# RWKV score products in quarter-array tiles: halves of the weights' tokens, and K against A and r in one product

## The chip, the cores and the metric

One core of one Trainium2 chip runs the whole model: four layers on one sequence of 256 tokens with 2048 channels. The metric is the device time of one execution in microseconds. The kernel before was run three times: 2886.83 us in the median, 2881.13 to 2887.49.

## The reference, cut to what matters

Layers 0 and 3 are RWKV-7 mixers with 32 heads of 64 channels, layer 1 is gated linear attention, layer 2 a state-space mixer. The change touches the RWKV mixer alone. Its recurrence is

```
def step(state, inp):
    r_t, k_t, v_t, w_t, kk_t, a_t = inp
    removal = jnp.einsum('bhvk,bhk->bhv', state, kk_t)
    state = (state * w_t[:, :, None, :]
             - jnp.einsum('bhv,bhk->bhvk', removal, kk_t * a_t)
             + jnp.einsum('bhv,bhk->bhvk', v_t, k_t))
    return state, jnp.einsum('bhvk,bhk->bhv', state, r_t)
```

The kernel computes it in two chunks of 128 tokens. Within a chunk it needs, for each head, four 128 x 128 matrices of products between tokens, each a sum over the head's 64 channels: the removal rows against the removal columns (B with A), B with r, K with A and K with r, where A, B, K and R are the four scaled vectors that the code keeps in one tile, `abkp`.

## The kernel before, in words

All activations lie transposed: channels on the 128 partitions, 256 tokens along the free axis. The large projections (`proj`, `jobs`, `prods`, line 393) take a 512 KB block of weights at a time, split it into a high and a low part (ScalarE line 338, VectorE line 340) and make three products of 256 columns for each 128 x 128 block into the PSUM tile `acc`. They fill most of the time of TensorE.

An RWKV layer goes through its 2048 channels in 8 units of 256 channels, that is of 4 heads. A unit holds two tiles of 128 channels (index q), each with two heads (index h: partitions 0 to 63 and 64 to 127), and two chunks of 128 tokens (index c). Two stages matter here, each running beside a projection:

- `rwkv_first` (beside the projection to k) makes A, B and K, writes them to DRAM, and calls `gram` once for B with A: four entries, (c, q). VectorE scales the result into `LT` (line 769), and `unit_inverse` inverts it with many small products (lines 982 to 1024).
- `rwkv_second` (beside the projection to r) loads A, B, K and the decay back into `abkp`, multiplies r into the fourth part (line 807), and calls `gram` three times: once for B with R (four entries, (c, q); masked on VectorE at line 823) and once for each chunk in `prep` for K with A and R (four entries: A q0, A q1, R q0, R q1; masked at line 845). The masked matrices `G` are the weights of the products at lines 864, 891 and 892.

`gram` (line 776) takes a two-bank PSUM tile, one bank for each h. For each entry and each h it issues one float32 product (line 785): the 64 channels of the head are the contracted rows, 128 tokens of s are the weights, 128 tokens of t are the moving columns. One call is 8 products; the trace shows two weight loads and two matmul records for each float32 product, so 16 records. There are 4 calls in a unit, 8 units in a layer and 2 such layers: 64 calls.

The source's order isn't the order of the queues: the Tile framework schedules the whole program with `schedule_with_timeline_sim=True`, so products of different parts are mixed on TensorE's queue by priority and by the times that its planner assumes. Semaphores are set from the data. A call of `gram` can so be cut into several pieces with other products between them. DMA traffic of this part is on GpSimd's queue (loads of `abkp`, `rv`, `Tt`) and SyncE's (stores); the weight blocks are on SyncE's.

Of the kernel before, what the change touches and what calls it, by code (L numbers as in the profile page):

```python
# [129 lines left out]
class Kern:  # L130
# [555 lines left out]
    def rwkv_first(self, i, j, un, kps, lora, ra):  # L686
# [7 lines left out]
        NCH, C, H = 2, 128, 64  # L694
# [5 lines left out]
        def v2(t):  # L700
            return t[:, 0:512].rearrange("p (q t) -> p q t", q=2)
# [7 lines left out]
        kT, tha, S = abk[:, 0, :], abk[:, 1, :], abk[:, 2, :]  # L709
# [4 lines left out]
        for n, (nm, dst, b) in enumerate((("dec", thd, self.hw0), ("iclr", tha, self.ha0))):  # L714
            ps = self.b1()
            for q in range(2):
                nc.tensor.matmul(ps[:, q * T:(q + 1) * T], w2[0:LORA, n, q * P:(q + 1) * P], lora[nm][0:LORA],
                                 start=True, stop=True)
# [20 lines left out]
        ps = self.b1()  # L739
# [25 lines left out]
        Lf = ra.tile([P, 8 * C + 16], F32, name="LT", bufs=3)  # L765
        nc.gpsimd.memset(Lf[:, 8 * C:], 0.0)
        LT = Lf[:, 0:8 * C].rearrange("p (m t) -> p m t", t=C)
        for h, g in enumerate(self.gram([(v2(tha), v2(kT), c, q) for c in range(NCH) for q in range(2)])):
            nc.vector.tensor_tensor(out=LT[:, 4 * h:4 * h + 4, :], in0=g,
                                    in1=n2[:, 4 * h:4 * h + 4].unsqueeze(2).broadcast_to([P, 4, C]), op=ALU.mult)  # L770
        Tt = self.unit_inverse(LT, Lf, ra)
# [4 lines left out]
    def gram(self, which):  # L776


        C, H = 128, 64
        both = self.g2()  # L780
        ps = [both[:, h, :] for h in range(2)]
        for n, (s, t, c, q) in enumerate(which):
            for h in range(2):
                r = slice(H * h, H * h + H)
                self.nc.tensor.matmul(ps[h][:, n * C:(n + 1) * C], s[r, q, c * C:(c + 1) * C], t[r, q, c * C:(c + 1) * C],  # L785
                                      start=True, stop=True)
        return [p.rearrange("p (n t) -> p n t", t=C) for p in ps]

    def rwkv_second(self, i, j, un, spill, kept, rb, last):
# [3 lines left out]
        NCH, C, H = 2, 128, 64  # L793
# [3 lines left out]
        abkp = rb.tile([P, 4, 2, T], F32, name="abkp")  # L797
        nc.gpsimd.dma_start(out=abkp, in_=kept[0].rearrange("p w (q t) -> p w q t", q=2))
        Ac, Bc, Kc, Rc = (abkp[:, w] for w in range(4))
# [12 lines left out]
        ps = self.b1()  # L812
# [4 lines left out]
        def Gt():  # L817
            return rb.tile([P, 4, C], F32, name="G", bufs=7)

        GBR = []  # L820
        for h, g in enumerate(self.gram([(Bc, Rc, c, q) for c in range(NCH) for q in range(2)])):
            GBR.append(Gt())
            nc.vector.tensor_tensor(out=GBR[h], in0=g, in1=self.c("kmask", C).unsqueeze(1).broadcast_to([P, 4, C]),
                                    op=ALU.mult)
        def prep(c):


            tk = rb.tile([P, 3, 2, P], F32, name="tk", bufs=3)
            for w0, ws in ((0, (Bc, Kc)), (2, (vT,))):
                if w0 == 0 and c == NCH - 1:  # L830
                    continue
                ps = self.b1()
                for w, src in enumerate(ws):
                    for q in range(2):
                        o, t = ps[:, (2 * w + q) * P:(2 * w + q + 1) * P], src[:, q, c * C:(c + 1) * C]
                        if w0 == 2:
                            nc.tensor.matmul(o, t, self.c("cen"), start=True, stop=True)
                        else:
                            nc.tensor.transpose(o, t, self.c("ident"))
                n = len(ws)  # L840
                nc.scalar.copy(out=tk[:, w0:w0 + n, :, :].rearrange("p w q t -> p (w q t)"), in_=ps[:, 0:n * 2 * P])
            G = []
            for h, g in enumerate(self.gram([(Kc, t, c, q) for t in (Ac, Rc) for q in range(2)])):
                G.append(Gt())
                nc.vector.tensor_tensor(out=G[h].rearrange("p (w q) t -> p w q t", w=2),
                                        in0=g.rearrange("p (w q) t -> p w q t", w=2),
                                        in1=self.c("kmask").rearrange("p (w t) -> p w t", w=2).unsqueeze(2)
                                        .broadcast_to([P, 2, 2, C]), op=ALU.mult)
            return tk, G
        first = prep(0)  # L850
        yield

        yb = self.b3()
        St = self.St[un % 2]
        for c in range(NCH):
            tk, G = prep(c) if c else first
            ps = self.b2()
            for q in range(2):
                if c:
                    nc.tensor.matmul(ps[:, q * P:(q + 1) * P], Ac[:, q, c * C:(c + 1) * C], St[:, q].rearrange("p h v -> p (h v)"),  # L860
                                     start=True, stop=False)
                for h in range(2):
                    n = 2 * q + h
# [3 lines left out]
            ps = self.b2()  # L867
# [6 lines left out]
            if c < NCH - 1:  # L874
                ps = self.b2()
                for n, (q, h) in enumerate(QH):
                    o = ps[HS[h], q * H:(q + 1) * H]
# [6 lines left out]
            for q in range(2):  # L884
# [3 lines left out]
                for h in range(2):  # L888
                    n = 2 * q + h
                    o = yb[:, c * T + n * H:c * T + (n + 1) * H]  # L890
# [12 lines left out]
        ps = self.b1()  # L903
# [562 lines left out]
```

## Time and profile before

| what | value |
|---|---|
| median of three runs | 2886.83 us (2881.13 to 2887.49) |
| the profiled execution's own time | 2881.41 us |
| its span, first to last instruction | 2879.4 us |
| TensorE busy (matmul) | 2691.4 us, 93% |
| VectorE busy | 2213.7 us, 77% |
| ScalarE busy | 1392.7 us, 48% |
| mean granted TensorE clock, 1 is 2.4 GHz | 0.959 |

The profiled execution is 5.4 us (0.19%) under the median of the runs. Busy time counts a stretch once even where records overlap. A matmul record reaches some 0.2 us beyond its stream of columns, so the pace of products is read from starts: from the start of a group to the start of the next.

### The profile page before, as it was taken

The page shows a single profiled execution, that of the slowest core. Times are in us where ns is not written, and L with a number is a line of the kernel's source. Part 1 is how long each engine was busy: PE and PEld are TensorE (multiplying, and loading weights), DVE is VectorE, ACT ScalarE, POOL GpSimd, SP SyncE. Part 2 cuts the span into 40 slices and gives each one's busy share as a digit, 9 for nine tenths or more (in the row PEclk, how much of TensorE's full clock was granted, in tenths as well). Part 3 has the DMA queues.
Part 4 walks back from the last instruction along what each step waited for, and adds up shares of the span by engine and source line. Part 5 has one row for each costly group of instructions (what it writes and reads, how often), then busy time and mean ns, then how long its engine had stood idle before and what let it go on. Part 6 is the DMA issues. An engine that isn't in the chain of part 4 may idle for free.

```text
span 2879.4 us, 62022 instructions
## 1 busy us (share of the span) xinstructions
PE 2691.4 (93%) x25074; PEld 2533.2 (88%) x25074; DVE 2213.7 (77%) x3918; ACT 1392.7 (48%) x2315; POOL 153.8 (5%) x298
## 2 busy tenths in 40 slices
PE   6899899999977999998998999999889989999997
PEld 4789899998967899987898999999779989899997
DVE  5778777878788988877888787887678888565666
ACT  3475655333335544444544454554357666452333
POOL 0011110101000000000000000000001011110100
PEclk8899889999998999999999999999999989999999
DMA  9876558978586888975775767666557765684633
GB/s 341 313 239 198 165 162 285 352 270 293 178 287 222 315 296 295 321 257 196 280 264 191 233 221 232 220 212 223 180 170 242 228 197 184 194 299 160 206 118 114
DMA packets 239118, 673.55 MB, mean 234 GB/s; under 512 B 72272, under 2 KB 78416, under 8 KB 235760
## 3 DMA queue, kind: packets, MB, share of 16 engines
q1 hardware_dynamic: 217904, 580.84, 59.8%
q0 software_dynamic: 20928, 88.75, 8.6%
q8 instruction: 197, 3.23, 0.5%
q14 instruction: 89, 0.73, 0.1%
HBM read 620.66 MB, written 48.82 MB: 233 GB/s over the span
## 4 chain that ended last, share of the span: by engine, by line
PE 72%; DVE 10%; DMA 10%; issue 3%; ACT 2%; SPq 2%; POOL 0%; DVEq 0%; ACTq 0%; POOLq 0%
PE acc L393 56%; DMA raw<-in_ada_w 3%; DVE L L340 3%; PE g L785 2%; PE pv L393 2%; DVE adaacc L304 2%; ACT H L338 1%; DMA raw<-in_rwkv_w_in 1%; DMA raw<-in_rwkv_w_out 1%; DMA dx<-bd 1%; PE b L892 1%; PE b L869 1%; DMA raw<-in_gla_w_in 1%; PE b L891 1%; PE b L864 1%
## 5 line engine op out<-in xcount | busy, mean ns | idle before, releaser
L393 PE MATMUL acc<-xs,H 128*128 128x256 f32 x8480 | 1631.3, 291 | 32.0 <-ACT H L338 8.4
L393 PEld LDWEIGHTS acc<-xs,H 128*128 128x128 f32 x8480 | 1359.7, 196 | 61.7 <-ACT H L338 10.9
L393 PE MATMUL acc<-xs,L 128*128 128x256 f32 x4240 | 1228.9, 290 | 18.2 <-DVE L L340 17.9
L338 ACT CAST H<-raw 128x1024 fp32r<-128x1024 f32 (+1 forms) x706 | 718.2, 1018 | 862.0 <-PE acc L393 636.1
L340 DVE TENSOR_TENSOR L<-raw,H 128x1024 fp32r<-128x1024 f32 (+1 forms) x706 | 834.1, 1184 | 249.0 <-ACT H L338 233.9
L393 PEld LDWEIGHTS acc<-xs,L 128*128 128x128 f32 x4240 | 828.3, 195 | 31.9 <-DVE L L340 23.4
L304 DVE SCALAR_TENSOR_TENSOR adaacc<-raw,cact,adaacc 128x1024 f32<-128x1024 f32 x300 | 384.0, 1280 | 111.5 <-DMA raw<-in_ada_w 109.5
L393 PE MATMUL acc<-ys,H 128*128 128x256 f32 x1536 | 292.2, 290 | 10.1 <-DVE ys L409 3.8
L393 PEld LDWEIGHTS acc<-ys,H 128*128 128x128 f32 x1536 | 244.7, 194 | 20.7 <-issue 7.4
L393 PE MATMUL acc<-ys,L 128*128 128x256 f32 x768 | 221.1, 288 | 0.0
L393 PEld LDWEIGHTS acc<-ys,L 128*128 128x128 f32 x768 | 149.0, 194 | 3.2 <-issue 3.2
L551 ACT ACTIVATE hn<-x,mod,omu 128x256 f32<-128x256 f32 x192 | 113.4, 599 | 2.9 <-DVE xm L554 1.4
L431 DVE SCALAR_TENSOR_TENSOR x<-acc,mod,x 128x256 f32<-128x256 f32 x192 | 83.7, 478 | 33.3 <-PE acc L393 33.1
L393 PE MATMUL acc<-H,xs 128*128 128x256 f32 x512 | 97.4, 290 | 0.9 <-ACT vt L1072 0.7
L554 DVE SCALAR_TENSOR_TENSOR xm<-x,par,hn 128x256 f32<-128x256 f32 x192 | 88.9, 478 | 1.4 <-ACT hn L551 0.3
L393 PEld LDWEIGHTS acc<-H,xs 128*128 128x128 f32 x512 | 82.7, 198 | 2.5 <-issue 1.2
L393 PE MATMUL acc<-L,xs 128*128 128x256 f32 x256 | 73.7, 289 | 0.0
L785 PE MATMUL g<-abkp 64*128 64x128 f32 x768 | 68.6, 294 | 1.8 <-DVE abkp L807 1.7
L408 ACT CAST xs<-xm 128x256 fp32r<-128x256 f32 x128 | 50.9, 400 | 34.1 <-DVE xm L554 31.8
L785 PEld LDWEIGHTS g<-abkp 64*128 64x128 f32 x768 | 53.4, 189 | 14.2 <-issue 6.2
L1278 DVE SCALAR_TENSOR_TENSOR cva<-cvp,hcw,cva 128x256 f32<-128x256 f32 x144 | 65.1, 478 | 0.0
L278 DVE SCALAR_TENSOR_TENSOR adaacc<-raw,cact,adaacc 128x512 f32<-128x512 f32 x56 | 42.0, 749 | 28.1 <-DMA raw<-in_ada_w 23.4
(358 smaller groups left out, 3138.4 us busy)
## 6 DMA issues: line engine op xcount, KB each, us to landing
raw<-in_ada_w SPq DMA_DIRECT2D x384, 512.0 KB, 4.9
raw<-in_rwkv_w_in SPq DMA_DIRECT2D x256, 512.0 KB, 4.8
raw<-in_ssd_w_in SPq DMA_DIRECT2D x128, 512.0 KB, 4.3
raw<-in_gla_w_in SPq DMA_DIRECT2D x96, 512.0 KB, 5.2
raw<-in_ssd_w_out SPq DMA_DIRECT2D x64, 512.0 KB, 4.0
raw<-in_rwkv_w_out SPq DMA_DIRECT2D x48, 512.0 KB, 4.4
abkp<-kd POOLq DMA_DIRECT2D x16, 1024.0 KB, 7.8
raw<-in_gla_w_out SPq DMA_DIRECT2D x32, 512.0 KB, 4.9
```

Source lines behind the costliest of these rows:

```text
L278: nc.vector.scalar_tensor_tensor(out=acc, in0=raw[:, u, :], scalar=self.cact[:, k:k + 1], in1=acc, op0=ALU.mult, op1=ALU.add)
L304: nc.vector.scalar_tensor_tensor(out=acc, in0=raw, scalar=self.cact[:, k:k + 1], in1=acc, op0=ALU.mult, op1=ALU.add)
L338: nc.scalar.copy(out=hi, in_=raw[:, a:a + n])
L340: nc.vector.tensor_tensor(out=lo, in0=raw[:, a:a + n], in1=hi, op=ALU.subtract)
L393: self.nc.tensor.matmul(ps, lhs, rhs, start=first and part == 0 and w is hi, stop=last and w is lo)
L408: nc.scalar.copy(out=t[:, 0, :], in_=src)
L431: nc.vector.scalar_tensor_tensor(out=self.x[:, t, 1:], in0=ps[:, u, :], scalar=gate[:, t:t + 1], in1=self.x[:, t, 1:], op0=ALU.mult, op1=A ...
L551: nc.scalar.activation(t1, x[:, k, 1:], AF.Identity, scale=self.omu[:, col:col + 1], bias=self.mods[(i, 0)][:, k:k + 1])
L554: done[k] = nc.vector.scalar_tensor_tensor(out=xm, in0=x[:, k, 0:T], scalar=self.p("rwkv_mu", col), in1=t1, op0=ALU.mult, op1=ALU.add)
L785: self.nc.tensor.matmul(ps[h][:, n * C:(n + 1) * C], s[r, q, c * C:(c + 1) * C], t[r, q, c * C:(c + 1) * C], start=True, stop=True)
L864: nc.tensor.matmul(ps[:, n * H:(n + 1) * H], G[h][:, q, :], tk[:, 2, q, HS[h]], start=not c, stop=not c or h == 1)
L1278: nc.vector.scalar_tensor_tensor(out=a, in0=src[:, k:k + T], scalar=w[k], in1=a, op0=ALU.mult, op1=ALU.add)
```

## The change

`gram` now gives every product a quarter of the array. Before, an entry was two products, one for each head, with 128 tokens of s as weights. Now it is four: for each head (h, the contracted rows) and each half of s's tokens (u, 64 weights' columns and 64 output partitions). The order is (u, h) = (0, 0), (1, 1), (1, 0), (0, 1). Output banks and places are as before: bank h, partitions by u.

The moving side gets one more axis, so that one product can stream several parts of `abkp`. For K with A and R, `abkp[:, 0::3]` is parts 0 and 3, and a product has 2 x 128 = 256 moving columns; the entries go from four to two. For B with A and B with R the axis has length 1 and a product keeps its 128 columns.

So a call for K has 2 x 4 = 8 products of 64 rows x 64 weights' columns with 256 moving columns (before: 8 of 64 x 128 with 128). A call for B with A or with R has 4 x 4 = 16 products of 64 x 64 with 128 moving columns (before: 8 of 64 x 128 with 128). Nothing else is edited.

```diff
-        for h, g in enumerate(self.gram([(v2(tha), v2(kT), c, q) for c in range(NCH) for q in range(2)])):
+        for h, g in enumerate(self.gram([(v2(tha), v2(kT).unsqueeze(1), c, q) for c in range(NCH) for q in range(2)])):
...
         for n, (s, t, c, q) in enumerate(which):
-            for h in range(2):
-                r = slice(H * h, H * h + H)
-                self.nc.tensor.matmul(ps[h][:, n * C:(n + 1) * C], s[r, q, c * C:(c + 1) * C], t[r, q, c * C:(c + 1) * C],
-                                      start=True, stop=True)
+            for u, h in ((0, 0), (1, 1), (1, 0), (0, 1)):
+                r, o = slice(H * h, H * h + H), slice(H * u, H * u + H)
+                tr = t[r, :, q, c * C:(c + 1) * C]
+                nt = tr.shape[1]
+                to = ps[h][o].rearrange("p (w n t) -> p w n t", w=nt, t=C)[:, :, n, :]
+                self.nc.tensor.matmul(to, s[r, q, c * C + H * u:c * C + H * u + H], tr, start=True, stop=True)
...
-        for h, g in enumerate(self.gram([(Bc, Rc, c, q) for c in range(NCH) for q in range(2)])):
+        for h, g in enumerate(self.gram([(Bc, abkp[:, 3:4], c, q) for c in range(NCH) for q in range(2)])):
...
-            for h, g in enumerate(self.gram([(Kc, t, c, q) for t in (Ac, Rc) for q in range(2)])):
+            for h, g in enumerate(self.gram([(Kc, abkp[:, 0::3], c, q) for q in range(2)])):
```

## Rows read from the trace of the kernel before

**Rows 1.** The page's busy times and its chain that ended last, by engine.

```profile
PE 2691.4 (93%) x25074; PEld 2533.2 (88%) x25074; DVE 2213.7 (77%) x3918; ACT 1392.7 (48%) x2315; POOL 153.8 (5%) x298
...
PE 72%; DVE 10%; DMA 10%; issue 3%; ACT 2%; SPq 2%; POOL 0%; DVEq 0%; ACTq 0%; POOLq 0%
```

**Rows 2.** Busy time by stretch: the RWKV stages of both layers, and their sum.

```profile
520.00:840.00 320.00, 303.79 (x2643) 286.21 (x2642) 249.87 (x421) 100.84 (x158) 26.39 (x48) 0.98 0.76 271
...
2470.00:2790.00 320.00, 313.44 (x3294) 294.24 (x3295) 202.87 (x381) 122.22 (x207) 35.28 (x66) 0.99 0.59 200
sum 1070.00, PE 1024.49 PEld 964.77 DVE 784.26 ACT 478.67 POOL 112.20; mean PE 256.12 PEld 241.19 DVE 196.06 ACT 119.67 POOL 28.05
```

**Rows 3.** Line 785 (gram): its matmul records, and their busy time over the same stretches.

```profile
L785 PE MATMUL g<-abkp x768: 272/272/579, 522.4 to 2782.9; 64*128 64x128 f32 x192
...
L785 PE MATMUL g<-abk x256: 272/272/580, 232.0 to 2450.1; 64*128 64x128 f32 x128
...
sum 1070.00, PE 84.97 PEld 66.49; mean PE 21.24 PEld 16.62
```

**Rows 4.** Timeline of TensorE: gram in one piece, and a piece of eight.

```profile
530.25 0.97 PEld L785 LDWEIGHTS g<-abkp 64*128 64x128 f32 x16
530.25 1.16 PE L785 MATMUL g<-abkp 64*128 64x128 f32 x16
...
531.34 0.39 PE L393 MATMUL acc<-xs,L 128*128 128x256 f32 x1
...
524.68 0.71 PE L785 MATMUL g<-abkp 64*128 64x128 f32 x8
525.32 0.38 PE L393 MATMUL acc<-xs,L 128*128 128x256 f32 x1
```

**Rows 5.** Timeline of TensorE: the state-space layer's products in two column halves (128*64).

```profile
1426.49 0.39 PE L1362 MATMUL b<-M,xc 128*64 128x128 f32 x4
...
1427.80 0.39 PE L1362 MATMUL b<-M,xc 128*64 128x128 f32 x4
...
1428.67 1.09 PE L1364 MATMUL b<-ce,xd 128*64 128x128 f32 x16
1429.69 0.39 PE L393 MATMUL acc<-xs,L 128*128 128x256 f32 x1
```

**Rows 6.** Timeline of TensorE: float32 products of 256 columns, whole array and four column quarters.

```profile
523.00 0.70 PE L814 MATMUL b<-rv,cst 128*128 128x256 f32 x2
523.63 0.48 PE L785 MATMUL g<-abkp 64*128 64x128 f32 x2
...
502.64 0.64 PE L310 MATMUL mx<-adaacc,cst 128*32 128x256 f32 x8
503.20 0.39 PE L393 MATMUL acc<-xs,H 128*128 128x256 f32 x1
```

**Rows 7.** Timeline of TensorE: 32*32 products with the same rows, mixed, and one kind alone.

```profile
299.85 0.19 PE L1012 MATMUL b<-P,T 32*32 32x32 f32 x1
...
300.20 0.19 PE L1012 MATMUL b<-P,T 32*32 32x32 f32 x1
300.32 0.38 PE L393 MATMUL acc<-xs,H 128*128 128x256 f32 x1
...
303.26 0.69 PE L1010 MATMUL b<-T,P 32*32 32x32 f32 x16
303.88 0.38 PE L393 MATMUL acc<-xs,L 128*128 128x256 f32 x1
```

**Rows 8.** Who reads gram's result, who waits for it, and who waits for line 807.

```profile
L845 DVE TENSOR_TENSOR G<-g,cst x64: 675/681/692, 534.9 to 2783.9; 128x512 f32<-128x512 f32 x64
...
PE g L785: 14.4, 17
...
PEld g L785: 2.2, 3
PE g L785: 1.7, 2
```

## The prediction

> **What bounds the kernel now.** I read the page first, then the stretches, then line 785 by itself, then the timeline product by product. The page shows an engine that is nearly full: TensorE is busy 93% of the span and holds 72% of the chain that ended last [rows 1]. In the four RWKV stretches that contain every call of gram it is fuller still, 1024.5 of 1070 us or 96%, with VectorE at 73% [rows 2]. So time saved on TensorE there should come through at about 0.95 of its size, and time added costs the same share. The granted clock is 0.98 and 0.99 in the two long stretches [rows 2], which is the upper level, 2.4 GHz, nearly throughout; I take all durations at that level.
>
> Gram has 768 + 256 = 1024 matmul records and 85.0 us of busy time [rows 3]. How that splits is read from two pieces. Sixteen records go from 530.25 to the next product's start at 531.34, 1.09 us; eight go from 524.68 to 525.32, 0.64 us [rows 4]. The difference, 0.45 us for eight records, is 56 ns for each record, and what is left, 1.09 - 16 x 0.056 = 0.19 us, is paid once for each piece: the first weight load, and the emptying of the array before the next kind of product. The busy times of the two pieces, 1.16 and 0.71 us, are 0.26 us over the same 56 ns for each record. So 85.0 = 1024 x 0.056 + pieces x 0.265, which gives 104 pieces for the 64 calls: some calls are cut by other products, 40 times in all.
>
> **The change, part by part.**
>
> *The work itself.* The array does as many multiplications as before. A record of 128 columns in half the array (64 x 128) becomes two in a quarter, or one in a quarter with twice the columns. A gain can only come from the way the tiles fill and empty, and a loss if quarters don't run side by side.
>
> *Do column halves run side by side?* The state-space layer has float32 products of 128 columns in column halves (128*64). From 1426.49 to 1427.80, six groups of four records pass in 1.31 us, 54.6 ns for each [rows 5], the pace that two at a time give, as in gram. Sixteen in one piece take 1428.67 to 1429.69, 1.02 us; less 16 x 0.0546 that is 0.15 us for the piece. Against gram's 0.19 this is 0.04 us less, and the difference I put down to the first load, which has 64 columns of weights in place of 128.
>
> *Do four run side by side, with 256 columns?* On the whole array two records of 256 columns take 523.00 to 523.63, 0.63 us, that is about 0.20 us for the piece and 0.216 for each. In four column quarters eight records take 502.64 to 503.20, 0.56 us [rows 6]: two rounds of 0.216 and 0.13 for the piece. Four records cost what one costs.
>
> *Do two run side by side that share their rows?* This is what gram never did: (u, h) = (0, 0) and (1, 0) both read partitions 0 to 63. The nearest rows are the 32*32 products of the inverse. Lines 1010 and 1012 both contract partitions 32 to 63, into different PSUM partitions. From 299.85 to 300.20 twelve of line 1012 pass, with twelve of line 1010 between them; that is eleven intervals in 0.35 us, 32 ns for a pair. Line 1010 alone takes 303.26 to 303.88, 0.62 us for sixteen; less about 0.12 for the piece, 31 ns for one [rows 7]. So two tiles with the same rows pass in the time of one. The trace has no 64*64 case of this, so I keep both ends: side by side, as these rows show, or two at a time, which doubles the rounds.
>
> *A call for K* (32 of them) becomes four rounds of four records of 256 columns: 0.15 + 4 x 0.216 + 0.02 for the staggered start of four = 1.03 us, against 1.09. *A call for B with A or R* (32) becomes eight rounds of four records of 128: 0.15 + 8 x 0.109 + 0.02 = 1.04 us. The saving is 0.06 and 0.05 us, together 3.5 us if each call is one piece. The 40 further pieces each get the shorter load less the stagger, 0.02 us, 0.8 us. That is 4.3 us on TensorE, and 4.1 at 0.95. The other end of the unknown: with two at a time a call takes 4 x 0.216 or 8 x 0.109 us more, 0.87, and 64 calls 56 us.
>
> *What is added.* The 32 calls for B have 8 more products each, 512 more records and as many loads. They stream beside the others and are in the sum above; their issue has no row of its own, and the 32*32 rows, at 16 ns for each record [rows 7], bound it under the 27 ns that a quarter of a round of 109 ns leaves. Nothing in DMA, ScalarE or VectorE is added or moved: the masks of line 845 keep their 0.68 us for the same 128 x 512 [rows 8].
>
> *The new wait.* A product of K with A now waits for line 807 as well, since it streams R with it. Behind it on TensorE's queue would stand the projection. B with R comes first in the same unit and waits for line 807 already; TensorE's waits for that line are 2.2 + 1.7 us in the whole span [rows 8]. I take nothing for it; if that cover went, it could double these, at most 4 us.
>
> *Latency.* VectorE stood idle 14.4 us in 17 stops for gram [rows 8]. Each now ends 0.05 us earlier, 0.9 us at most.
>
> **The sum** is 4.1 + 0.9 = 5.0 us. From the profiled execution's 2881.4 us that is 2876.4. That execution lies 5.4 us under the median of the runs, so against the median of 2886.8 I expect **2882 us**, 0.17% less. A measurement of this kernel can tell some 0.2%, 5.8 us, from no change, so the forecast lies just inside what can't be told.
>
> *A rule that speaks against it.* If a weight load could not pass beside a running product of the same rows, gram before would already take a load and a product in turn. It doesn't: its sixteen loads take 0.97 us in all, and the products follow at 56 ns each, 112 for two in parallel, although in each half every load has the same rows as the product ahead of it [rows 4]. The Trainium skill, in "TensorE: Matmul & The Clock Gate", Part 3, under what overlaps and what doesn't, says that a weight load overlaps with products in flight only when the row groups differ. By that rule, the trace disagrees before the change; it would have to hold for quarter tiles alone.
>
> **The rivals.**
>
> *The pieces become fewer or more.* The planner sets the order anew for the whole program, with twice the products in the calls for B and longer ones in the calls for K. For fewer speaks that a call for K has two entries in place of four, so fewer places to cut. If all 40 cuts went, at 0.17 us each (0.15 + 0.02), 7 us more would be saved: 2882 - 7 = **2875 us**.
>
> *Cuts that leave quarters alone* (the other side). A call for K that is cut after one product runs two records of 256 columns with three quarters of the array empty. That costs 0.17 for the piece and 2 x 0.216 for rounds hardly filled, 0.6 us, where a cut before cost 0.19 and at most two records' 0.11. Against the 5 us saved and the 5.8 that can be told, it decides from 18 such cuts in the 32 calls; one in each would give 2882 + 19 = **2901 us**. For it speaks that 40 cuts exist now; against it, that the busy time of the pieces fits full pairs closely, so cuts mostly fall between entries.
>
> *Tiles with the same rows run in turn.* Then 56 x 0.95 = 53 us are added: **2935 us**. Only that no 64*64 pair was seen speaks for it; rows 7 speak against it.
>
> *Loads are not hidden in quarter tiles.* Each round would then show its load of 64 columns. From rows 4 and 5, 64 columns less cost 0.04 us of the fixed part, so I take 0.05: 32 x 8 + 32 x 4 = 384 rounds, 19 us, **2900 us**. By the Trainium skill's rule above this is what would come.
>
> *Nothing comes through.* Where the projection beside gram waits for VectorE or for a weight block, TensorE's 4 us are lost again: **2887 us**. TensorE's 96% speaks against it.
>
> **How the numbers follow.** The forecast has 0.50: its own range is 2876 to 2888, by what a new order of the queues moves (one cut is 0.17 us, a few waits of the projection 1 us each); of this 0.16 falls beyond 0.2% faster, 0.33 within, 0.01 slower. Fewer pieces 0.22, faster. Lonely quarters 0.12, of which 0.11 slower and 0.01 within. The same rows in turn 0.05, slower. Loads not hidden 0.05, slower. Nothing comes through 0.06, within. Together: faster 0.38, within 0.40, slower 0.22. The range goes from 2871 (no cuts left and a few waits gone) to 2901, which takes in the loads and the lonely quarters; what is left out is the 2935 us and the tails, under 2 in 10.
>
> **What would show it.** Right: line 785 has 512 + 512 records of 128 columns and 512 of 256, all 64*64; an uncut call for K lasts about 1.03 us to the next product's start and an uncut call for B 1.04, with starts in fours; busy time of the line falls under 85 us; TensorE's share in the RWKV stretches stays at 96%. Wrong: an uncut call near 1.9 us (turns), near 1.3 for K and 1.5 for B (loads), or calls near 1.03 us in more than 120 pieces with the line's busy time above 90 us. If calls last what I say and the time still moves by more than 10 us, the cause is the order of the other work, which my sum doesn't hold.

## The result, and the profile after

The changed kernel takes 2909.63 us in the median of four runs (2908.33 to 2914.86), the kernel before 2885.12 beside it (2881.13 to 2887.49): a ratio of 1.0093, with a 95% interval of 1.0068 to 1.0118. It is 24.5 us slower. The forecast was 2882, its range ended at 2901, and slower had a chance of 0.22: the prediction was wrong in its sign and its range. The profiled execution after took 2908.33 us with a span of 2906.0.

The page after, where it answers to [rows 1]; then the two costliest lines of TensorE (busy, mean ns, idle ahead of them and its main releaser):

```profile
span 2906.0 us, 63046 instructions
...
PE 2697.5 (93%) x25586; PEld 2519.3 (87%) x25586; DVE 2211.1 (76%) x3918; ACT 1392.7 (48%) x2315; POOL 154.0 (5%) x298
...
PE 70%; DVE 12%; DMA 11%; issue 4%; ACT 2%; SPq 1%; POOL 0%; DVEq 0%; ACTq 0%; POOLq 0%
...
L393 PE MATMUL acc<-xs,H 128*128 128x256 f32 x8480 | 1634.4, 291 | 40.3 <-DVE xs L409 10.4
...
L393 PE MATMUL acc<-xs,L 128*128 128x256 f32 x4240 | 1232.1, 291 | 21.3 <-DVE L L340 21.1
```

TensorE has the 512 further records (25586 against 25074) and 6.1 us more busy time, about a quarter of the 26.6 us by which the span grew; the other 20.5 us are idle time of TensorE (208.5 us for 188.0). In the chain TensorE has two points less, VectorE two and DMA one more: there is more waiting. The projection's own two groups waited 40.3 and 21.3 us; before, 32.0 and 18.2. The mean granted clock of the span is 0.954, before 0.959.

**Where the time went.** The same two stretches (first RWKV layer; the two middle layers) of the kernel before, and then of the kernel after. The columns are the stretch, its length, busy time and instructions of PE, PEld, DVE, ACT and POOL, then the granted clock, the DMA share and GB/s.

```profile
200.00:1000.00 800.00, 746.63 (x7518) 697.47 (x7518) 638.87 (x1119) 379.69 (x665) 62.83 (x119) 0.96 0.73 248
1000.00:2200.00 1200.00, 1143.77 (x9276) 1094.17 (x9276) 963.65 (x1600) 586.25 (x871) 13.32 (x22) 0.97 0.70 237
```

```profile
200.00:1000.00 800.00, 733.66 (x7600) 672.35 (x7598) 618.96 (x1093) 370.27 (x648) 62.74 (x119) 0.94 0.70 237
1000.00:2200.00 1200.00, 1143.68 (x9272) 1093.10 (x9273) 965.29 (x1597) 580.34 (x858) 12.27 (x20) 0.97 0.70 240
```

In the middle layers TensorE's busy time is the same to a tenth of a microsecond. In the first stretch every engine is busy for less of the 800 us, at a granted clock of 0.94 for 0.96. I set the two traces side by side by the k-th product of the projection's line 393, which has 16416 in both: product 1200 comes 2.6 us later after the change (258.5 for 255.9), product 1600 17.2 us (363.5 for 346.3), product 2800 27.3 us (613.5 for 586.2). At the end it is 26.5. For four fifths of the products between, the difference is 22 to 27 us; for short stretches, in the two RWKV layers above all, it moves out to 18 or 40. So in these two executions nearly all is lost in the first RWKV layer, and most of it before the second stage.

**The tiles themselves did what they should.** Line 789 (gram) after: records, shortest, median and longest in ns, first and last start, shapes of some.

```profile
L789 PE MATMUL g<-abkp x1024: 269/376/685, 538.7 to 2803.2; 64*64 64x128 f32 x86, 64*64 64x256 f32 x85
...
L789 PE MATMUL g<-abk x512: 269/269/418, 233.9 to 2465.5; 64*64 64x128 f32 x171
```

Timeline of TensorE after: a call for B in one piece, a call for K in one piece, and a call for K in two (start, busy, line, tiles, count).

```profile
263.15 1.10 PE L789 MATMUL g<-abk 64*64 64x128 f32 x32
264.18 0.39 PE L393 MATMUL acc<-xs,L 128*128 128x256 f32 x1
...
550.48 1.09 PE L789 MATMUL g<-abkp 64*64 64x256 f32 x16
551.50 0.39 PE L393 MATMUL acc<-xs,L 128*128 128x256 f32 x1
...
616.71 0.66 PE L789 MATMUL g<-abkp 64*64 64x256 f32 x6
617.30 0.66 PE L909 MATMUL b<-cst,ysq 128*128 128x128 f32 x4
```

A call for B takes 264.18 - 263.15 = 1.03 us, a call for K 551.50 - 550.48 = 1.02, against 1.09 for both in [rows 4]. Cut, the call for K pays 0.59 us for six records, and the other ten, further on, 1.00 (not shown here): 1.59 instead of 1.02.

### The profile page after: what moved, and what is told of

The parts are those of the page before. It is cut to its first block, busy times and chain, and to the rows that moved or that the text cites. A ratio compares the mean times of both kernels' runs of the same rounds, so it can differ in the third digit from the quotient of the medians.

```text
span 2906.0 us, 63046 instructions
## 1 busy us (share of the span) xinstructions
PE 2697.5 (93%) x25586; PEld 2519.3 (87%) x25586; DVE 2211.1 (76%) x3918; ACT 1392.7 (48%) x2315; POOL 154.0 (5%) x298
## 4 chain that ended last, share of the span: by engine, by line
PE 70%; DVE 12%; DMA 11%; issue 4%; ACT 2%; SPq 1%; POOL 0%; DVEq 0%; ACTq 0%; POOLq 0%
PE acc L393 55%; DMA raw<-in_ada_w 5%; DVE L L340 3%; DVE adaacc L304 2%; PE pv L393 2%; PE g L789 2%; DMA raw<-in_rwkv_w_in 1%; ACT H L338 1%; DMA raw<-in_gla_w_in 1%; PE b L895 1%; DMA raw<-in_rwkv_w_out 1%; PE b L894 1%; PE b L872 1%; PE b L867 1%; DMA dx<-bd 1%
## 5 line engine op out<-in xcount | busy, mean ns | idle before, releaser
L393 PE MATMUL acc<-xs,H 128*128 128x256 f32 x8480 | 1634.4, 291 | 40.3 <-DVE xs L409 10.4
L393 PE MATMUL acc<-xs,L 128*128 128x256 f32 x4240 | 1232.1, 291 | 21.3 <-DVE L L340 21.1
L789 PE MATMUL g<-abkp 64*64 64x256 f32 (+1 forms) x1024 | 68.5, 347 | 3.3 <-DVE abkp L810 2.7
L278 DVE SCALAR_TENSOR_TENSOR adaacc<-raw,cact,adaacc 128x512 f32<-128x512 f32 x56 | 41.9, 748 | 27.8 <-DMA raw<-in_ada_w 23.1
L393 PE MATMUL pv<-xs,H 128*128 128x256 f32 x256 | 55.6, 312 | 3.7 <-ACT H L338 3.7
```

Of the source, the lines that this page charges most:

```text
L278: nc.vector.scalar_tensor_tensor(out=acc, in0=raw[:, u, :], scalar=self.cact[:, k:k + 1], in1=acc, op0=ALU.mult, op1=ALU.add)
L393: self.nc.tensor.matmul(ps, lhs, rhs, start=first and part == 0 and w is hi, stop=last and w is lo)
L789: self.nc.tensor.matmul(to, s[r, q, c * C + H * u:c * C + H * u + H], tr, start=True, stop=True)
```

## The experiments

Two explanations stand against each other. The order theory says that the planner, given other products, set all the queues anew, and that this order costs the time. The tile theory says that the quarter tiles themselves cost it.

Each kernel's ratio is to runs of the kernel before on the same chip (medians 2880.2, 2880.0, 2883.1 and 2879.6 us in the four groups, e1 to e4, e5 to e8, e9 to e12, e13 to e16). Each was executed six or twelve times; in brackets stands the 95% interval. "Products 1200 to 1600" are those of the projection's line, as above. A trace shows one execution, which need not be a typical one.

The instrument for most of them: the planner's order is read out for one kernel, engine by engine, and another kernel (or the same) gets dependences that order and do nothing else, so that every engine's queue stands as in that list. Gram's products go where the other kernel has its gram products.

```diff
-            Kern(ctx, tc, A, out)
+            hold_order(nc, tc, Kern(ctx, tc, A, out).calls)
...
+    for text in ORDER:
+        prev = None
+        for s in np.cumsum(np.frombuffer(zlib.decompress(base64.b85decode(text)), "<i4")):
...
+                if prev is not None:
+                    tc.add_manual_dep(i, prev.name, info, reason="the other kernel's order")
+                prev = i
```

**e9_control_held**: the kernel before, held in its own order. What does the instrument cost?

> Control: the kernel before, unchanged, with its own order written down and held as in the other held kernels. If holding an order costs nothing, as all readings of the held kernels assume: ratio 0.999 to 1.001. If the held kernels carry an offset of their own (all so far read 1.001 or more): 1.001 to 1.003, and then the 0.30% of the new tiles in the old order is partly that offset.

2883.46 us, ratio 0.9999 [0.9981, 1.0016]: nothing.

**e1_new_tiles_old_order**: the changed kernel, with ORDER from the kernel before.

> The changed kernel, with every engine's queue held to the order of the kernel before (edges of order alone; only gram's products differ, and they stand where gram's stood). Order theory (line 785/789 costs the same 85 us in both traces, and the 24 us are waits and half-clock stretches that the newly planned order brings): 2881 to 2886 us, ratio to before 0.998 to 1.000. Tile theory (quarter tiles themselves cost time, by an emptier array, a lower clock or waits of their own): 2900 to 2910 us, ratio 1.006 to 1.009.

2888.42 us, 1.0030 [1.0015, 1.0045]: about a third of what the change costs, with the other instructions in their old places. It lies between the two ranges that were expected.

**e2_old_tiles_new_order**: the kernel before, with ORDER from the changed kernel.

> The converse: the kernel before, with every engine's queue held to the changed kernel's order. Order theory: 2905 to 2912 us, ratio 1.007 to 1.010, with waits of TensorE in the first RWKV stage where the changed kernel has them. Tile theory: 2881 to 2888 us, ratio 0.999 to 1.001.

2894.73 us, 1.0068 [1.0043, 1.0094]. Not one product differs from the kernel before, and yet most of the loss is there, though less than the 2905 to 2912 us that the order theory expected. Its trace loses as the changed kernel's does, 17.9 us by product 1600 and 27.5 by product 2800; but the traced execution is the longest of the six, 2911.69 us, 17 above their median. The two parts, 0.68% and 0.30%, add up to 0.98%, beside 0.93% measured for the change; the intervals allow from 12 to 27 us for the order and from 4 to 13 for the tiles.

**Which tiles carry the 0.3%?** Two kernels with one kind of call in quarter tiles, held in the old order.

```diff
-            for h, g in enumerate(self.gram([(Kc, t, c, q) for t in (Ac, Rc) for q in range(2)])):
+            for h, g in enumerate(self.gram([(Kc, abkp[:, 0::3], c, q) for q in range(2)])):
...
-        for h, g in enumerate(self.gram([(Bc, Rc, c, q) for c in range(NCH) for q in range(2)])):
+        for h, g in enumerate(self.halves([(Bc, Rc, c, q) for c in range(NCH) for q in range(2)])):
```

That is e7 as against the kernel before (K in quarters, B as before, by a copy of the old function, `halves`; the call for B with A is edited like that for B with R); e8 is the reverse.

> Quarter tiles with 256 columns for K with A and R alone, all queues in the order of the kernel before. New tiles in the old order cost 0.30% (0.15 to 0.45). If that comes from K's products (a cut leaves a lone product of 2 x 216 ns in a quarter of the array, and A waits for r): ratio 1.002 to 1.003. If from the calls for B: 1.000.

> Quarter tiles with 128 columns for B with A and B with R alone, all queues in the order of the kernel before. If the 0.30% comes from their 512 further records or from cut pieces: ratio 1.002 to 1.003. If it comes from K's products: 0.999 to 1.001.

e7: 2882.56 us, 1.0012 [0.9994, 1.0030], no difference that can be told. e8: 2889.05, 1.0036 [1.0016, 1.0056]. This points to B's calls, with their 512 further records, for the part that does not come from the order; the two intervals overlap, so it is not shown. In e8's profile gram's own time, from each piece's start to the next product's, is 83.0 us, less than the 84.0 of the control e9. Why B's tiles should cost time is open.

**The same part of the change, planned anew**: quarter tiles in the first stage only (B with A), in the second only (B with R, and K), and for K only. The edits are those above, without the held order.

> Quarter tiles in the call for B with A alone (rwkv_first), the three calls of rwkv_second as before; the order is planned anew. The traces lose 18 us by the end of the first layer's first stage (products 1200 to 2400 of line 393) and 11 us in the last layer's. Order theory: as the new order starts in that stage, most of the loss stays, 2895 to 2910 us, but no part of it lies in gram's own products. Tile theory with the cost in the second stage's 256-column products: 2885 us.

> The converse: rwkv_first's call as before, quarter tiles in rwkv_second alone; planned anew, with the order unchanged until the end of the first layer's first stage. Order theory: the first stage loses nothing, and what is left is the 9 us of the handover to the second stage or less, 2880 to 2895 us. Tile theory with the cost in the 256-column products: 2900 us or more.

> Quarter tiles for K with A and R alone, planned anew; the same products in the old order read 1.0012 (0.9994 to 1.0030). If a newly planned order moves the time by itself, whatever the products: a ratio outside 0.998 to 1.004, to either side (quarter tiles for rwkv_second alone, planned anew, read 1.008). If a new plan costs only where B's calls are cut differently: 1.000 to 1.003.

e3: 2884.02 us, 1.0016 [1.0000, 1.0033]. e4: 2901.49, 1.0080 [1.0053, 1.0108]. e12: 2876.23, 0.9982 [0.9966, 0.9999]. With the changed kernel these are four plans for nearly the same work, from 0.2% faster to 0.9% slower. e4 loses its time later than the changed kernel, mainly between products 2800 and 3200: it isn't one bad decision that all of them share. e12 is the only version of the change whose whole interval lies under 1, by 0.0001; among sixteen intervals that can be chance, and the ratio outside 0.998 to 1.004 that was expected of a new plan was just missed.

Both expectations of the order theory failed for e3 and e4: it had 2895 to 2910 us for e3 and 2880 to 2895 for e4. It took the cost to sit in the first stage, and e3 speaks against that. In their traces e3 and the changed kernel have the same order of TensorE's products, with the same quarter tiles, up to product 2529, beyond the first stage. e3 is 13.9 us behind the kernel before at product 1600 and 16.4 at 2800, and yet its time is only 0.16% longer, at most 0.33%. What it shares with the changed kernel therefore costs it at most 0.33%, where the change costs 0.68 to 1.18%, unless e3's own plan behind it wins time back. Either way the first stage alone does not set the changed kernel's loss.

**Where in the order is the cost?** The work of the kernel before, with the new order in one stretch and the old in the rest.

> Old tiles; the queues in the changed kernel's order up to the middle of the program (through the first RWKV layer), then in the order of the kernel before. The trace of old tiles in the new order is 28 us behind by product 2800 of line 393 and keeps that. If the first layer's order holds the cost: 2895 to 2903 us, ratio 1.005 to 1.008. If it is spread: 1.002 to 1.004.

> The converse: old tiles, the order of the kernel before through the first RWKV layer, the changed kernel's order after it. If the first layer's order holds the cost: ratio 0.999 to 1.002. If it is spread: 1.003 to 1.005.

> Old tiles; the order the planner made for the changed kernel up to product 1200 of the projection's line (the input stage, about 256 us), the old order from there. Theory (the first RWKV stage's order costs the time): no change, 2878 to 2888 us, ratio 1.000 +- 0.002, and products 1200 to 1600 take 88 to 93 us. Rival (what goes wrong is set up ahead of the stage, by the order of the weight loads and input work): 2890 us or more, and those products take 98 us or more.

> Old tiles; the new order up to product 1600, the old one from there. Theory (the time lost in the first stage stays lost): 2891 to 2898 us, ratio 1.003 to 1.006, products 1200 to 1600 in 100 to 105 us. Rival (a loss in the stage is regained when the later work stands in the old order): 2879 to 2887, with the same 100 to 105 us in the stage but the difference gone by product 2800.

> Old tiles; the new order between products 1200 and 1600 alone, the old one before and after. Theory: as the kernel with the new order up to 1600, 2891 to 2898 us, ratio 1.003 to 1.006, the stage in 100 to 105 us. Rival (the stage needs what stands ahead of it too): within 0.2% of the kernel before and the stage in 88 to 93 us.

> Old tiles; the old order up to product 1200, the new one from there to the end. Theory: as the whole new order, 2891 to 2900 us, ratio 1.004 to 1.009. Rival (what stands ahead of the first stage sets the loss): within 0.2% of the kernel before.

| new order in | us | ratio and interval |
|---|---|---|
| e10, first RWKV layer | 2896.47 | 1.0045 [1.0028, 1.0063] |
| e11, last RWKV layer | 2879.21 | 0.9997 [0.9978, 1.0017] |
| e13, up to product 1200 | 2883.96 | 1.0018 [1.0002, 1.0034] |
| e14, up to product 1600 | 2895.38 | 1.0050 [1.0035, 1.0066] |
| e15, products 1200 to 1600 | 2893.80 | 1.0047 [1.0026, 1.0068] |
| e16, from product 1200 on | 2902.83 | 1.0077 [1.0055, 1.0099] |

The order after the first RWKV layer costs nothing that can be told, the order ahead of product 1200 little (0.18%). With e10 and e16, which came out a little above its 2891 to 2900 us, this puts the cost between product 1200 and the end of the first RWKV layer. A new order of the 400 products from 1200 on, 90 us of 2880, makes the kernel half a per cent slower. Three things keep this from being the whole account. e14 missed its 100 to 105 us: the stretch took 95.7. e14 and e15 both go on losing after product 1600, 12 and 10 us by product 2800, where the queues stand in the old order again. There is a stop of 8.3 us just behind the place where the orders are joined (line 718, for the tanh of line 721), which is not in the changed kernel; but at product 1800 both are less than 2 us further behind than at 1600, so it does not account for those 12 and 10. And e3 has the new order in this stretch too and loses hardly anything in the end. So a new order from 1200 to 1600 with the old one behind it is shown to cost time; what the stretch costs in the changed kernel is not.

The stretch from product 1200 to 1600 in six traces, in the columns above: the kernel before, the control e9, e13, then the kernel after, e2 and e15.

```profile
255.90:346.30 90.40, 85.36 (x1146) 80.17 (x1145) 76.10 (x175) 53.34 (x108) 10.93 (x21) 0.93 0.59 180
```

```profile
257.30:348.50 91.20, 86.00 (x1147) 80.42 (x1146) 77.50 (x179) 53.56 (x110) 11.17 (x21) 0.93 0.59 184
```

```profile
258.60:345.30 86.70, 83.05 (x1138) 77.54 (x1137) 73.03 (x163) 50.88 (x103) 10.19 (x20) 0.96 0.59 181
```

```profile
258.50:363.50 105.00, 95.44 (x1267) 89.06 (x1266) 75.14 (x173) 54.80 (x111) 11.62 (x23) 0.85 0.52 158
```

```profile
261.20:364.20 103.00, 93.18 (x1202) 87.16 (x1201) 70.97 (x160) 54.44 (x110) 11.59 (x23) 0.87 0.52 156
```

```profile
261.20:364.40 103.20, 93.30 (x1202) 87.31 (x1203) 71.41 (x161) 54.44 (x109) 12.36 (x24) 0.87 0.52 155
```

The same stretch in e14 and e3, which stand in the new order there as well:

```profile
255.40:351.10 95.70, 87.41 (x1203) 81.62 (x1202) 70.67 (x161) 54.07 (x109) 11.59 (x23) 0.93 0.54 168
```

```profile
258.40:360.20 101.80, 91.82 (x1267) 85.16 (x1265) 74.92 (x173) 54.66 (x111) 11.59 (x23) 0.88 0.54 163
```

The first three stand in the old order there: 87 to 91 us, clock 0.93 to 0.96. The other five stand in the new one: 96 to 105 us, clock 0.85 to 0.93. The traces of e2 and e15 come from executions 17 and 15 us above their medians, that of e13 from one 9 us under it, so the gap between the two sets is in part one of executions. e2 and e14 have the same products in the same order up to product 1600, and they take 103.0 and 95.7 us here. TensorE's busy time makes 5.8 of these 7.3 us, and the clock is at half for 27.3 us in e2 and 13.7 in e14. So much of the low clock in this stretch is not set by the order.

Read e2 against the control, which have the same products: the stretch is 11.8 us longer, of which TensorE is busy 7.2 and idle 4.6 more. The 7.2 have two sources. The new order does 55 more records of other lines between the same two products of the projection (1202 for 1147), so it takes up some later work, which is no loss; and at the lower clock the same product takes longer. In the trace, the granted clock stands at 0.5 (1.2 GHz) for 12.0 us of the control's stretch and for 27.3 of e2's. Three products of the projection take 0.64 us at half and 0.36 at full clock (rows below), so of the 15.3 us more at half up to 0.28/0.64 is lost, 6.7 us, in this execution. VectorE meanwhile does 19 instructions fewer (160 for 179) in a longer time.

**One such place, in the trace after.** ScalarE's queue, then TensorE's; the bracket gives idle time just ahead and what ended it.

```profile
293.80 1.09 ACT L738 ACTIVATE thd<-abk,par 128x256 f32<-128x256 f32 x2 [2.04 <-DVE abk L723]
294.97 0.21 ACT L733 ACTIVATE Pt<-mid 128x4 f32<-128x4 f32 x1
295.63 0.63 ACT L734 ACTIVATE Pt<-abk 128x512 f32<-128x512 f32 x1 [0.45 <-DVE abk L727]
...
296.29 0.63 ACT L735 ACTIVATE abk<-abk 128x512 f32<-128x512 f32 x1
296.94 0.84 ACT L720 ACTIVATE abk<-b,ha 128x256 f32<-128x256 f32 x2
```

```profile
297.84 1.56 PE L742 MATMUL b<-cst,thd 128*128 128x2 f32 x8 [3.42 <-ACT abk L720]
299.26 0.56 PE L393 MATMUL acc<-xs,H 128*128 128x256 f32 x1
...
300.47 0.63 PE L393 MATMUL acc<-xs,H 128*128 128x256 f32 x2
300.89 0.41 PE L393 MATMUL acc<-xs,L 128*128 128x256 f32 x1
...
308.65 0.40 PE L393 MATMUL acc<-xs,H 128*128 128x256 f32 x2
308.89 0.28 PE L393 MATMUL acc<-xs,L 128*128 128x256 f32 x1
```

The small product of line 742 stands in TensorE's queue ahead of the projection and waits 3.42 us. By the trace the last thing to come was the second tanh of line 720 (`abk`), and that stood in ScalarE's queue behind the squares and exponentials of the same unit, which wait for VectorE's line 723 and 727. After the stop, the granted clock is at 0.5 from 298.2 to 308.5 (10.2 us): three products of the projection take 0.64 us from 300.47 to the next start at 301.11, and 0.36 from 308.65 to 309.01, once it is up again. That is ten microseconds at half speed behind a stop of 3.4. Line 742 has two further stops in this stage, of 2.0 and 0.8 us, and behind them the clock is at 0.5 for 6.8 and 10.2 us. That the stops bring on the low clock is my reading; in the last layer a stop of 0.8 us of the same line (at 2312.7) has no low clock in the 30 us behind it.

**Is that one wait the cause?** In e5 the tanh stands ahead of the squares in ScalarE's queue, in the 12 of 16 units where it stood behind, with all else in the new order; e6 does the same to the kernel before in the old order.

The edit is in the list of the order alone: of its five parts only ScalarE's differs from that of e2 (for e6, from that of e9). In the traces the first tanh stands behind the unit's first square in 12 of 16 units before and after the change, and in none in e5 and e6.

> The changed kernel in its own order, with one edit on ScalarE's queue alone: in the 12 of 16 units where the two tanh of the learning-rate product (iclr) stand behind the unit's squares and exponentials, they stand ahead of them. In the changed kernel's trace the product behind them on TensorE (the norms' sums, L742) waits 15.8 us for these tanh in 10 stops, each followed by half-clock stretches. If the place of such instructions in the queues is where the time goes: most of the 15.8 us vanishes and with it part of the half clock, 2885 to 2902 us, ratio to before 1.000 to 1.006. If the queues' order is only a sign and the tiles or the DMA set the time: 2905 to 2912 us.

> The same edit in the kernel before (12 units as well; its L742 waits 14.2 us for these tanh in 6 stops). Order theory: faster than both kernels, 2865 to 2878 us, ratio 0.994 to 0.999. If another wait takes the place at once: no change.

e5: 2909.27 us, 1.0104 [1.0081, 1.0127], no gain; e6: 2884.65, 1.0013 [0.9999, 1.0027], none either. The edit did its work. What line 742 waited for, after, and the same line (743) in e5, over the whole span (matmuls and weight loads counted each; then the matmuls' waits alone, after):

```profile
  ACT abk L720: 15.8, 10
  ACT thd L738: 2.6, 2
```

```profile
  ACT thd L739: 1.7, 2
```

```profile
PE b L742 <- ACT abk L720: 7.5, 5, 3.4
```

So the 15.8 us of the expectation count each stop twice, once for the weight loads and once for the matmuls: TensorE stood 7.5 us in five stops, and not each was followed by a low clock. These 7.5 us are gone. The stretch from product 1200 to 1600 is shorter too (100.6 us, at half clock for 22.6; after, 105.0 and 30.7), but the whole time is not. In the first stage of e5 (255 to 365 us) TensorE now waits at other places:

```profile
PE b L994 <- issue: 2.3, 1, 2.3
PE b L1011 <- ACT P L1012: 2.1, 1, 2.1
PE b L988 <- DMA Tn<-xd: 2.0, 1, 2.0
PE b L1011 <- DVE Tn L995: 1.8, 1, 1.8
```

So the theory of one late tanh fell. My reading, not shown, is that the three engines wait for each other in turn in this stage, so that another wait takes the place of the one removed. Two rows of ScalarE's waits between products 1200 and 1600, of the kernel before and then of the one after, go with it (total, times, longest):

```profile
ACT H L338 <- PE acc L393: 10.7, 9, 3.0
...
ACT thd L738 <- DVE abk L723: 5.6, 2, 3.7
```

```profile
ACT H L338 <- PE acc L393: 15.7, 9, 3.0
ACT thd L738 <- DVE abk L723: 10.0, 4, 4.1
```

## Why the prediction was wrong, step by step

**What bounds the kernel: right.** TensorE does, and where it is held up the time goes with it: of the 26.6 us between the two traced spans 20.5 are more idle time of TensorE and 6.1 more busy time, the half clock included. One sign failed: TensorE's share was to stay as it was, and from product 1200 to 1600 it fell from 94% to 91%.

**Four quarter tiles run side by side, also two that share rows: right.** An uncut call has the predicted 1.03 us (K, measured 1.02) and 1.04 (B, 1.03). The rival of tiles in turn would have shown 1.9 us and is out.

**Loads hidden: right.** That rival would have shown near 1.3 us for K and 1.5 for B. The rule against the change, in the Trainium skill's "TensorE: Matmul & The Clock Gate", Part 3 (a load passes beside running products only where the row groups differ), is therefore not borne out by quarter tiles either: 16 records of 256 columns, each with a load whose rows the running tiles use, pass in 1.02 us. The Trainium skill's "TensorEngine Tiling (Array Packing)", under "The Solution", counts the 64×64 mode as four independent tiles, and that agrees with the 1.02 and 1.03 us.

**The 4.3 us saved on TensorE: nearly right, but it did not come through.** Summed over its pieces from start to the next product's start, gram took 85.3 us before and 85.5 after, in 104 and 105 pieces. Its busy time, over two stretches that hold all its records, before and then after:

```profile
200.00:1000.00 800.00, 44.49 (x512) 35.38 (x512) 0.96 0.73 248
2200.00:2860.00 660.00, 46.68 (x512) 35.59 (x512) 0.98 0.59 195
```

```profile
200.00:1000.00 800.00, 45.59 (x768) 25.27 (x768) 0.94 0.70 237
2200.00:2860.00 660.00, 42.73 (x768) 24.72 (x768) 0.97 0.61 200
```

91.2 us fell to 88.3, so at best 3 us came. It also shows a slip of mine: the 85.0 us of [rows 3] came from stretches that hold 960 of the 1024 records, so they did not contain every call of gram. The count of 104 pieces that I worked out from it is nevertheless what the trace has, and that is luck: the full 91.2 would have given 128, since pieces at the lower clock or with a stop are longer than the formula has it.

What ate the saving is not the tiles. Pieces with the same number of records mostly take the same time to 0.01 us. Seven pieces before and twelve after take over 0.1 us more, because they ran wholly or partly at half the clock or the product behind them waited; that excess is 3.7 us before and 7.6 after. Without it the pieces come to 81.6 and 77.9 us, a saving of 3.7. The longest, a call for K in one piece, lasts 3.31 us to the next product, which waits for ScalarE:

```profile
2740.59 1.09 PE L789 MATMUL g<-abkp 64*64 64x256 f32 x16
2743.90 0.51 PE L393 MATMUL acc<-xs,H 128*128 128x256 f32 x2 [2.21 <-ACT xs L408]
```

Cuts inside a group of four are in the 77.9. I took cuts to fall between entries, but of the 72 pieces before that are not a whole call, 36 end inside one. After, six of the 32 calls for K are cut, five of them inside a group, at 1.59 us instead of 1.02. That is the price of the lonely quarters (0.6 predicted, 0.57 measured), but 5 cuts, not the 18 from which that rival decides: 3 us, not 19.

**The 0.9 us of latency: wrong in sign.** VectorE's waits for gram, 14.4 us in 17 stops before, are 23.1 in 20 after. With the same tiles in the old order (e1) they are 13.6 in 18, so by these traces it goes with the order and not with the tiles.

**The new order of the queues: this is the step that failed.** I gave it "2876 to 2888, by what a new order of the queues moves (one cut is 0.17 us, a few waits of the projection 1 us each)". The order by itself moves 0.68% [0.43, 0.94], 12 to 27 us of 2880 (e2), some seven tenths of what the change cost; holding an order costs nothing (e9). I priced single waits and not what stands behind them. In the first stage of the changed kernel TensorE stood three times for line 720, 6.1 us together, and 27.3 us at a granted clock of 0.5 followed. The long stretches had 0.98 and 0.99 [rows 2], and I took all durations at the upper level from there; the stretch where the time first went had 0.93 before already, and I didn't look at it alone. That the order would be set anew was in my text as a reason for cuts, and my last sign named it: calls that last what I say and a time that still moves by more than 10 us. That is what came, but the sum gave it no price. It needed a rival of its own, with a price from what a differently ordered stage can lose.

**The new wait for line 807: nearly right to take nothing.** The 2.2 + 1.7 us of [rows 8] are mostly the same stops, seen from the weight loads and from the products, so they don't add. After, the two are 3.2 and 2.7 us: 1.0 us more.

**Nothing comes through**, the rival at 2887, agrees with what K alone gives in the old order (2882.6 beside 2880.0). All the tiles in the old order cost 0.3% (e1), which no term of the sum had.

**What stays open**: why the quarter tiles cost about 0.3% in an unchanged order, and B's, it seems, more than K's; which of the plan's decisions cost the time, and how much of it between product 1200 and the end of the first RWKV layer falls to which stage. One profile shows one execution, and single executions of e15 lie between 2882 and 2910 us; differences of a few us between two traces are no evidence. By product 1600 the traces of e2, e10 and e14, the same work in the same order until then, are 17.9, 12.9 and 4.7 us behind the kernel before.

## What to carry to other kernels

Where a planner sets the order of all queues, a change of a few instructions is two changes, and the second can be the larger: hold the order and measure the new instructions alone, then put the new order on the old instructions. A saving of 5 us on the busiest engine is not worth the forecast's first digit as long as the order is free to move by 20; it is worth trying several plans and keeping the best (the K tiles alone, planned anew, gave 2876.2 us beside 2883.1), after measuring the best one a second time, since it was picked from several. Read the clock and the waits of the stage where the engines wait for each other, not of the stretch where the bottleneck is fullest. And where one trace stands for a kernel, see first where its time lies among the executions.

## What the runs showed of the hardware

Quarter tiles of float32 in fours keep the pace of the halves: 16 records of 256 columns in 1.02 us and 32 of 128 in 1.03, though each pair shares rows and half as many weights are loaded at a time; the load's busy time fell from 71.0 to 50.0 us with 512 more loads. One to three 64*64 products of 256 columns between other lines (two to six records) take 0.57 to 0.59 us, so a cut inside a group costs as much as half a call. And a stop of 3.4 us was followed by 10.2 us at a granted clock of 0.5, in which the projection ran at 0.64 us for three products instead of 0.36.
